# A first image load whose reads span two rows (32 KB) in place of one (16 KB), without the build's mark, in a 3x3 convolution with a residual

## The chip, the cores and the metric

The kernel runs on one core of one Trainium2 chip. The metric is the device time of one execution in microseconds (us), as the median of several runs. "Slower" or "faster" is said of over 2%.

## The reference

Sixteen images of 64 channels and 64 x 64 pixels are convolved with 64 x 64 x 3 x 3 weights, padding 1, and a residual is added; all is float32.

```python
for b, co, ci, kh, kw in all indices:
    output[b, co] += weight[co, ci, kh, kw] * x_pad[b, ci, kh:kh+h, kw:kw+w]
return (output + residual).astype(np.float32)
```

In and out of HBM go 50.48 MB: images, residual and output of 16.78 MB each, and the weights.

## The kernel before

Images are handled in pairs: 128 partitions hold two images of 64 channels, one row of 16 KB each. ScalarE casts an image into a padded bfloat16 tile, TensorE multiplies, VectorE adds the residual, and SyncE stores. Two loads are moved to the very front of the program, ahead of its opening barrier (where all engines wait for each other): the first image pair on SyncE's DMA queue and the first residual pair on ScalarE's.

```python
def to_the_front(dma):
    ...
    front.insert(at, copy.replace(ins, ins=[fixed(a) for a in ins.ins], outs=[fixed(a) for a in ins.outs]))

for p in range(NPAIR):                      # SyncE
    if p >= NXR:
        nc.sync.wait_ge(s_half, 2 * (p - NXR) + 3)
    if p == 0:
        to_the_front(load_x(p))             # xr0 <- images 0 and 1
        nc.sync.dma_start(out=wraw[:, :], in_=w_rows[:, :]).then_inc(s_w, 16)
    else:
        load_x(p)
    ...                                     # residual pairs, then the stores

to_the_front(load_ro(0, nc.scalar))         # ScalarE: ro <- residual pair 0
for n in range(B):
    ...                                     # wait for the pair, cast image n
```

All DMAs of this program carry a mark, `ant_dge_precooked`, which the build puts on a DMA of a simple shape.

Of the kernel before, what the change touches and what calls it, by code (L numbers as in the profile page):

```python
# [15 lines left out]
def kernel(  # L16
# [64 lines left out]
    def load_x(p):  # L81
        return nc.sync.dma_start(out=xr[p % NXR][:, :], in_=x_bc[128 * p : 128 * p + 128, :]).then_inc(s_x[p % NXR], 16)

    def load_ro(i, e):
        pairs, cols, _ = RES[i]
        if i >= NR:
            e.wait_ge(s_r[i % NR], 16 * (i // NR))
        return e.dma_start(out=ro[:, pairs, cols], in_=res_bc[:, pairs, cols]).then_inc(s_r[i % NR], 16)
# [24 lines left out]
            )  # L113
        )

    def to_the_front(dma):



        def fixed(ap):  # L120
            t = ap.bass_ap.tensor.name
            return mybir.PhysicalAccessPattern(
                ap=ap.ap, offset=ap.bass_ap.offset, dtype=ap.dtype, memref=t, memsetref=t + "_set", bass_ap=ap.bass_ap
            )

        front = nc.main_func.blocks[0].instructions
        here = nc.cur_bb.bb.instructions
        ins = here.pop()
        assert ins.name == dma.ins.name
        at = next(i for i, e in enumerate(front) if e.engine == ins.engine)  # L130
        front.insert(at, copy.replace(ins, ins=[fixed(a) for a in ins.ins], outs=[fixed(a) for a in ins.outs]))


    blocks = ((0, 0, 0, 0), (1, 0, 0, 1), (1, 0, 1, 0), (0, 1, 1, 1), (0, 1, 0, 2), (1, 1, 1, 2))
# [7 lines left out]
    with tc.tile_critical(no_gpsimd_drain=True):  # L142

        for p in range(NPAIR):
            if p >= NXR:

                nc.sync.wait_ge(s_half, 2 * (p - NXR) + 3)
            if p == 0:
                to_the_front(load_x(p))
                nc.sync.dma_start(out=wraw[:, :], in_=w_rows[:, :]).then_inc(s_w, 16)  # L150
            else:
                load_x(p)
            for i, (_, _, behind) in enumerate(RES):
                if behind == p:
                    load_ro(i, nc.sync)
# [24 lines left out]


        to_the_front(load_ro(0, nc.scalar))
        for n in range(B):
            p, im = divmod(n, 2)
            hp = slice(64 * im, 64 * im + 64)
            x4 = xr[p % NXR].rearrange("q (j two w) -> q j two w", two=2, w=W)
            t = xp[n % NXP]
# [22 lines left out]
        for n in range(B):  # L210
            p, im = divmod(n, 2)
# [81 lines left out]
```

## Time and profile before

| | before |
|---|---|
| time, median of the first 3 runs (122.21 to 122.33) | 122.28 us |
| span of the profiled run | 120.6 us |
| first DMA packet starts, last one ends | 1.03 us, 119.21 us |
| first image cast starts | 11.54 us |
| first convolution matmul starts | 18.12 us |

The prediction below shows the page's lines and reads from them that the 16 DMA engines have no free time between the first packet and the last. In such a kernel the end is the time at which the engines get going plus the bytes over the rate.

### The profile page before, as it was taken

To read this page: it belongs to the slowest core of one execution; us is meant where nothing else is said; L and a number is where in the kernel's file an instruction comes from. 1 tells how busy PE (TensorE), PEld (TensorE's weight loads), DVE (VectorE), ACT (ScalarE), POOL (GpSimd) and SP (SyncE) were. 2 spreads that over 40 slices of the span, in tenths; PEclk is the share of its full clock that TensorE was granted. 3 is DMA by queue.
4 is the path that set the end of the run, shared out by engine and by line. 5 is a ranking of instruction groups with operands and counts; after the bars stand their busy time and mean duration, and the time that the engine had idled before them with its cause. 6 is when DMAs were issued, how large, how long until landed. Compare 5 with 4: busy or idle time off the path is not lost.

```text
span 120.6 us, 734 instructions
## 1 busy us (share of the span) xinstructions
PE 87.7 (73%) x389; PEld 10.7 (9%) x105; DVE 76.0 (63%) x40; ACT 63.1 (52%) x37; POOL 2.4 (2%) x16
## 2 busy tenths in 40 slices
PE   0000609999999999999999999999999999400000
PEld 0000300111101110101010101010101010000000
DVE  0000080039898898988989898898988989890000
ACT  4001999999988595875959578595800000000000
POOL 5200000000000000000000000000000000000000
PEclk9999999999999999999999999999999999995555
DMA  7999999999999999999999999999999999999994
GB/s 239 429 424 429 430 429 429 429 435 435 435 429 429 424 429 424 429 435 424 435 429 435 435 435 418 421 459 435 429 429 429 429 429 435 435 435 429 399 427 168
DMA packets 3808, 50.48 MB, mean 419 GB/s; under 512 B 352, under 2 KB 480, under 8 KB 480
## 3 DMA queue, kind: packets, MB, share of 16 engines
q1 hardware_dynamic: 3664, 48.38, 94.2%
q10 hardware_dynamic: 144, 2.10, 4.1%
HBM read 33.70 MB, written 16.78 MB: 419 GB/s over the span
## 4 chain that ended last, share of the span: by engine, by line
PE 71%; DVEq 2%; DVE 2%; issue 0%
PE ps L101 54%; PE ps L100 17%; DVEq L142 2%; DVE ro L220 2%
## 5 line engine op out<-in xcount | busy, mean ns | idle before, releaser
L220 DVE TENSOR_TENSOR ro<-ps,ro 64x2048 f32<-64x2048 f32 x32 | 73.2, 2288 | 17.7 <-PE ps L101 17.2
L101 PE MATMUL ps<-xp,wl 128*128 128x504 bf16 (+1 forms) x288 | 80.0, 388 | 0.2
L190 ACT CAST xp<-xr 64x2048 bf16<-64x2048 f32 x16 | 30.3, 1896 | 22.5 <-PE ps L101 13.1
L100 PE MATMUL ps<-xp,wl 128*128 128x504 bf16 (+1 forms) x92 | 35.9, 390 | 3.4 <-PEq L241 3.4
L194 ACT CAST xp<-xr 64x2048 bf16<-64x2048 f32 x16 | 30.4, 1898 | 0.4
L100 PEld LDWEIGHTS ps<-xp,wl 128*128 128x128 bf16 x96 | 9.5, 99 | 79.1 <-issue 79.1
L206 DVE CAST wl<-ps 32x192 bf16<-32x192 f32 x8 | 2.8, 348 | 14.9 <-PE ps L233 14.8
L233 PE MATMUL ps<-ident,wraw 128*32 128x128 f32 x9 | 2.1, 412 | 12.6 <-DMA wraw<-in_weight_dram 12.6
L233 PEld LDWEIGHTS ps<-ident,wraw 128*32 128x32 f32 x9 | 1.2, 137 | 13.0 <-issue 12.6
L190 ACT ACT_TABLE_LOAD x1 | 1.3, 1283 | 1.1 <-SPq L142 1.1
L199 ACT CAST wl<-ps 32x192 bf16<-32x192 f32 x4 | 1.2, 306 | 0.0
L177 POOL MEMSET xp<- 64x64 bf16 x4 | 0.6, 146 | 0.2
L176 POOL MEMSET xp<- 64x64 bf16 x4 | 0.6, 144 | 0.2
L165 POOL TENSOR_SCALAR_AFFINE_SELECT ident<-ident 128x128 f32<-128x128 f32 x1 | 0.3, 292 | 0.2 <-POOL ident L163 0.2
L179 POOL MEMSET wl<- 64x192 bf16 x1 | 0.3, 253 | 0.1
L178 POOL MEMSET wl<- 64x192 bf16 x1 | 0.3, 251 | 0.1
L163 POOL MEMSET ident<- 128x128 f32 x1 | 0.2, 204 | 0.7 <-SPq L142 0.7
L277 POOL MEMSET const-bfloat16-1.0<- 128x1 bf16 x1 | 0.1, 111 | 0.0
L277 POOL MEMSET const-uint8-127<- 128x1 uint8 x1 | 0.1, 111 | 0.0
L277 POOL MEMSET const-float32-1.0<- 128x1 f32 x1 | 0.1, 108 | 0.0
L277 POOL MEMSET const-float32-0.0<- 128x1 f32 x1 | 0.1, 103 | 0.2 <-issue 0.2
## 6 DMA issues: line engine op xcount, KB each, us to landing
xr<-in_x_dram SPq DMA_DIRECT2D x8, 2048.0 KB, 14.4
out_dram<-ro SPq DMA_DIRECT2D x3, 4096.0 KB, 19.2
ro<-in_residual_dram SPq DMA_DIRECT2D x2, 4096.0 KB, 20.7
ro<-in_residual_dram SPq DMA_DIRECT2D x2, 2048.0 KB, 18.1
ro<-in_residual_dram ACTq DMA_DIRECT2D x1, 2048.0 KB, 12.0
ro<-in_residual_dram SPq DMA_DIRECT2D x2, 1024.0 KB, 18.8
out_dram<-ro SPq DMA_DIRECT2D x1, 2048.0 KB, 13.7
out_dram<-ro SPq DMA_DIRECT2D x2, 1024.0 KB, 9.4
```

Of the source, the lines that this page charges most:

```text
L100: return e.matmul(out=out_, lhsT=lhsT, rhs=rhs, start=start, stop=stop, skip_group_check=True)
L101: return e.add_instruction(mybir.InstMatmult(name=nc.get_next_instruction_name(), engine=PE, ins=[e.lower_ap(rhs), e.lower_ap(lhsT)], outs ...
L142: with tc.tile_critical(no_gpsimd_drain=True):
L176: nc.gpsimd.memset(t[0:64, 0, :], 0.0).then_inc(s_id, 1)
L177: nc.gpsimd.memset(t[64:128, J, :], 0.0).then_inc(s_id, 1)
L190: i = nc.scalar.copy(out=t[64:128, 0:J, :], in_=x4[hp, :, 0, :])
L194: nc.scalar.copy(out=t[0:64, 1 : J + 1, :], in_=x4[hp, :, 1, :]).then_inc(s_pack, 1)
L199: i = nc.scalar.copy(**weight_block(h, *b))
L206: i = nc.vector.tensor_copy(**weight_block(h, *b))
L220: i = nc.vector.tensor_tensor(out=o4[hp, :, par, :], in0=psj[64 * par : 64 * par + 64, :, :], in1=o4[hp, :, par, :], op=ADD)
L233: i = nc.tensor.transpose(out=tp[0:32, t // 3, 128 * (t % 3) : 128 * (t % 3) + 128], in_=wraw3[:, :, t], identity=ident[:, :])
L277: nc = _bacc.Bacc("TRN2", target_bir_lowering=False, num_devices=1)
```

## The change

The intent: each DMA engine takes turns between the two queues, one packet each. If a packet of the image's queue carries 32 KB instead of 16, the image gets two thirds of the engines' time instead of half and arrives sooner. The new shape is not one that the build marks, so the change clears the mark on this one load.

```diff
-    def to_the_front(dma):
+    def to_the_front(dma, wide=False):
 ...
+        if wide:
+            (step, rows), *mid, (_, cols) = src.ap
 ...
+            src = copy.replace(src, ap=[[2 * cols, rows // 2], [1, 1], [1, 2 * cols]])
+            dst = copy.replace(dst, ap=[list(dst.ap[0]), [1, 1], list(dst.ap[-1])])
-        front.insert(at, copy.replace(ins, ins=[fixed(a) ...], outs=[fixed(a) ...]))
+        front.insert(at, copy.replace(ins, ins=[src], outs=[dst], ant_dge_precooked=not wide))
 ...
-                to_the_front(load_x(p))
+                to_the_front(load_x(p), wide=True)
```

More of the change, by code (lines that the diff above doesn't have):

```diff
@@ L114, in matmul, with fixed @@
         )
-    def to_the_front(dma):
-        def fixed(ap):
-            t = ap.bass_ap.tensor.name
-            return mybir.PhysicalAccessPattern(
-                ap=ap.ap, offset=ap.bass_ap.offset, dtype=ap.dtype, memref=t, memsetref=t + "_set", bass_ap=ap.bass_ap
-            )
+    def fixed(ap):
+        t = ap.bass_ap.tensor.name
+        return mybir.PhysicalAccessPattern(
+            ap=ap.ap, offset=ap.bass_ap.offset, dtype=ap.dtype, memref=t, memsetref=t + "_set", bass_ap=ap.bass_ap
+        )
+    def to_the_front(dma, wide=False):
         front = nc.main_func.blocks[0].instructions
@@ L129, in to_the_front @@
         assert ins.name == dma.ins.name
+        (src,), (dst,) = ins.ins, ins.outs
+        src, dst = fixed(src), fixed(dst)
+        if wide:
+            (step, rows), *mid, (_, cols) = src.ap
+            assert step == cols and all(n == 1 for _, n in mid)
+            src = copy.replace(src, ap=[[2 * cols, rows // 2], [1, 1], [1, 2 * cols]])
+            dst = copy.replace(dst, ap=[list(dst.ap[0]), [1, 1], list(dst.ap[-1])])
         at = next(i for i, e in enumerate(front) if e.engine == ins.engine)
-        front.insert(at, copy.replace(ins, ins=[fixed(a) for a in ins.ins], outs=[fixed(a) for a in ins.outs]))
+        front.insert(at, copy.replace(ins, ins=[src], outs=[dst], ant_dge_precooked=not wide))
     blocks = ((0, 0, 0, 0), (1, 0, 0, 1), (1, 0, 1, 0), (0, 1, 1, 1), (0, 1, 0, 2), (1, 1, 1, 2))
```

## The prediction

> **What bounds the kernel now.** I read the chain of waits first, because it names a suspect, and then the DMA rows, to see whether the suspect can be right. In the page, part 4 is the chain that ended last, part 2 the slices; the tenths of the DMA row are the mean busy share of the 16 DMA engines.
>
> ```profile
> PE   0000609999999999999999999999999999400000
> ...
> DMA  7999999999999999999999999999999999999994
> GB/s 239 429 424 429 430 429 429 429 435 435 435 429 429 424 429 424 429 435 424 435 429 435 435 435 418 421 459 435 429 429 429 429 429 435 435 435 429 399 427 168
> ...
> HBM read 33.70 MB, written 16.78 MB: 419 GB/s over the span
> ## 4 chain that ended last, share of the span: by engine, by line
> PE 71%; DVEq 2%; DVE 2%; issue 0%
> ```
>
> The chain says TensorE, but it ends near 108.9 us, when the last two stores are issued. What follows is transfer. The DMA row is at 9 from the second slice to the last but one, and PE is idle for the first four slices and the last five. I checked this on the records of single packets: all 16 engines run their packets back to back from 1.03 us (first packet) to 119.21 us (end of the last), each 16 KB packet in 611 ns, and no gap appears anywhere between. So the span is 1.03 us of start, 118.18 us of transfer, and 1.4 us of completion and closing barrier (119.21 to 120.61). The time of 122.28 us is 1.67 us more than the span.
>
> The second question is how much room the compute chain has before it would set the end. The last stores are issued at 108.88 and 109.28 us. The records show 4.19 MB whose packets start after 108.88 us; 2.10 MB of that are these two stores, so 2.10 MB stand ahead of them: at 0.43 MB per us, 4.9 us. Compute could end almost 5 us later before a DMA engine went idle, and ending earlier gains nothing.
>
> Then the start, where the change is. Stretches of the timeline (start, duration, engine, line):
>
> ```profile
> 0.00 0.38 SPq L82 DMA_DIRECT2D xr<-in_x_dram  x1
> 0.12 0.36 ACTq L88 DMA_DIRECT2D ro<-in_residual_dram  x1
> ...
> 1.11 0.33 SPq L150 DMA_DIRECT2D wraw<-in_weight_dram  x1
> ...
> 11.54 1.90 ACT L190 CAST xp<-xr 64x2048 bf16<-64x2048 f32 x1 [9.19 <-DMA xr<-in_x_dram]
> ...
> 12.61 2.08 PE L233 MATMUL ps<-ident,wraw 128*32 128x128 f32 x9 [12.61 <-DMA wraw<-in_weight_dram]
> 13.46 1.90 ACT L194 CAST xp<-xr 64x2048 bf16<-64x2048 f32 x1
> 14.80 2.89 DVE L206 CAST wl<-ps 32x192 bf16<-32x192 f32 x8 [14.80 <-PE ps L233]
> 15.27 1.26 ACT L199 CAST wl<-ps 32x192 bf16<-32x192 f32 x4
> ...
> 18.12 0.59 PE L100 MATMUL ps<-xp,wl 128*128 128x512 bf16 x1 [3.44 <-PEq L241]
> ```
>
> The reader is to see which of two loads opens the convolution. The image lands at 11.5 us and both its casts end at 13.46 + 1.90 = 15.36 us. The weights land at 12.47 us, are transposed until 14.69 us and cast by VectorE until 14.80 + 2.89 = 17.69 us; the first convolution matmul follows 0.43 us later. The weights set the first matmul; the image is 2.3 us early already.
>
> The packet records also show how the first image shares the engines with the first residual load, which ACT issues 0.12 us later. Each engine takes two image packets (starts at 1.03 to 1.56 and 2.10 to 2.64 us), then one of the residual (from 2.73), and from there strictly one and one. The image's eighth packet on the leading engine ends at 10.09 us; its completion write gets a turn only after another residual packet, at 10.69 us. The 128 weight packets (1152 bytes, 51 ns) run after that, 11.30 to 12.16 us.
>
> **What the Trainium skill says.** All four are on "DMA: Bandwidth & Descriptors".
> (1) Section "Queues, rings and completion order": each DMA engine goes round its queue rows at packet granularity. The trace agrees (the alternation above). If a 32 KB descriptor counts as one packet, the image takes two thirds of each round in place of a half.
> (2) Section "Bandwidth", "Where 436 GB/s comes from": the ceiling is 435 GB/s. The slices of the trace lie at 424 to 435, so there is no rate left to gain.
> (3) Section "Why a DMA increments its semaphore by 16 and not by 1": the number of engines k is the largest number up to 16 that divides the slowest dimension of both patterns. Here these become 64 on the source and 128 on the destination, so k stays 16. No trace shows this shape yet.
> (4) Section "Latency and other measured facts": first byte of an issue from SyncE or ScalarE some 600 ns. The trace has 0.65 us from the end of SyncE's first issue (0.38) to its first packet (1.03).
> I found nothing on these pages about the "precooked" mark that the change takes off this one load.
>
> **The change part by part.**
> *Removed:* per engine, 4 of 8 read descriptors of one load. Residual halves of 8 KB take 309 ns, and 2 x 309 - 611 = 7 ns, which I take as the fixed cost of a descriptor. 4 x 7 = 28 ns per engine: -0.03 us on the transfer, which is on the path.
> *Added:* every DMA in the program before carries the mark; this one loses it. What an unmarked issue costs on SyncE no run here shows. The eight image loads' issues last 327 to 562 ns; I take this spread, 0.24 us, as an estimate of what a slower issue may add. It would move the first packet from 1.03 to about 1.25 us. There is a cap: ACT's issue ends at 0.48 us, and with the same 0.65 us its packets could begin at 1.13 us, 0.10 us after the present start; the engines would then begin with residual packets instead. So the engines start 0.1 to 0.24 us later; I take +0.15 us, on the path. SyncE's longer issue also delays the opening barrier, hence the weights' issue (1.11 us), but their packets wait in the queue until after 9 us anyway: 0.
> *Moved:* with 32 KB rounds the image needs 8 packets of its own and about 3 of the residual, in place of 7 at the end of before (6 between, 1 before the completion write): 4 x 0.61 = 2.4 us less at most, 1.8 us if one more round slips in, minus the later start. I expect the image to land at about 9.5 us (9 to 10.3) instead of 11.5. The residual is not later: both loads together are the same 16 packets per engine. The weights stand behind the image in SyncE's queue. If they go round one descriptor at a time with the residual's remaining 4 or 5 packets, the last weight packet still follows the last residual packet, and they land at 12.3 to 12.7 us, as before. ScalarE then casts image 0 about 2 us sooner and waits for the transposes; VectorE still ends its weight casts near 17.7 us, and the first convolution matmul stays at 18.0 to 18.4 us. On the end: 0, for two reasons, as the weights gate the matmuls and the DMA engines gate the end.
> *Sum:* 122.28 + 0.15 - 0.03 + 0 = 122.40 us.
>
> **The rivals.**
> Compute sets the end, as the chain of waits suggests, and an image that lands 2 us earlier takes up to 2 us off: about 120.3 us. Against it: 4.9 us of queued transfer ahead of the last store, and no DMA gap in 118 us. Even if true, the weights hold the first matmul.
> The weights come earlier: if several weight descriptors go in one turn, they land near 10 us, and the first matmul moves to about 15.7 us. That is a real move of the compute chain, but the same 50.48 MB follow: 122.4 us again. The image loads that wait for ScalarE would be issued earlier into a queue that is never empty.
> The wide descriptor is bad for the engines: the two patterns differ in length, so the load runs at half its rate or on fewer engines. Its 2.1 MB cost 4.9 us of the 16 engines; at half rate, with the residual filling in only partly, 1 to 4 us would be lost: 123.5 to 126 us. For: no run here has such a shape. Against: the page's rule keeps 16 engines, and 16 KB packets already run at the ceiling.
> The unmarked issue is far slower, 1 us or more: the residual's 4.9 us of work is there to fill in, so the loss stays near 0.25 us: 122.5 us.
>
> **Range and chances.** Three of these ways end within 122.25 to 122.55 us; the spread of the runs of before (122.21 to 122.33) and the 0.4 us by which the engines' last packets differ (118.78 to 119.21) widen it. The range is 122.15 to 122.75 us. Faster by over 2% needs under 119.9 us, less than the transfer with its start and closing takes: 0.01. Slower by over 2% needs over 124.7 us, which only the bad-descriptor way gives: 0.02. Within 2%: 0.97.
>
> **What would show it.** The first packet at 1.1 to 1.3 us, and the last packet's end shifted by about the same; the DMA row still without a gap; 64 fewer packets, if a packet is a read descriptor; ScalarE's first cast at 9.3 to 10.4 us in place of 11.54; the transposes at 12.4 to 12.9 us; the first convolution matmul at 18.0 to 18.4 us. I am wrong if the time moves by more than 0.5 us either way, if a DMA slice in the first 12 us falls below 9, or if the first matmul moves with the image. The weakest step is the cost of the missing mark.

## The result, and the profile after

The changed kernel takes 122.79 us (median of 4 runs, 122.67 to 122.98), the kernel before 122.31 us in the same rounds. The ratio is 1.0042 with a 95% interval of 1.0024 to 1.0059. Ratios here are the mean time of one kernel's runs over that of the other's of the same rounds, so not quite the ratio of the medians quoted. It is within 2%, as forecast, but the time lies 0.04 us outside the range, and the rise is 0.48 us where 0.12 was named.

First the page's slice rows after. One slice is 3.03 us, and a packet is booked in the slice in which it starts.

```profile
DMA  6989999999999999999999999999999999999993
GB/s 179 514 357 387 447 433 433 433 433 433 428 433 433 428 433 433 433 433 433 433 428 433 433 433 398 433 458 433 433 428 422 433 428 433 433 428 433 409 422 160
DMA packets 3744, 50.48 MB, mean 417 GB/s; under 512 B 352, under 2 KB 480, under 8 KB 480
```

The engines are full from the second slice on. The digit of 8 in the third comes from the booking: with each packet's time spread over its duration, the records fill that slice. The loss lies at the left edge: the first slice has 179 GB/s where it had 239. The 64 packets that are missing (3744 after 3808) are the wide load's: 64 of 32 KB in place of 128 of 16 KB. The single 514 and 357 are no real rates: a 32 KB packet is booked whole where it starts.

Then the opening in the timeline after (start, duration, engine, line):

```profile
0.00 0.56 SPq L82 DMA_DIRECT2D xr<-in_x_dram  x1
0.12 0.38 ACTq L88 DMA_DIRECT2D ro<-in_residual_dram  x1
...
1.43 0.36 SPq L157 DMA_DIRECT2D wraw<-in_weight_dram  x1
...
11.77 1.90 ACT L197 CAST xp<-xr 64x2048 bf16<-64x2048 f32 x1 [9.10 <-DMA xr<-in_x_dram]
...
12.85 2.08 PE L240 MATMUL ps<-ident,wraw 128*32 128x128 f32 x9 [12.85 <-DMA wraw<-in_weight_dram]
...
15.04 2.89 DVE L213 CAST wl<-ps 32x192 bf16<-32x192 f32 x8 [15.04 <-PE ps L240]
15.49 1.26 ACT L206 CAST wl<-ps 32x192 bf16<-32x192 f32 x4
...
18.36 0.59 PE L100 MATMUL ps<-xp,wl 128*128 128x512 bf16 x1 [3.44 <-PEq L248]
```

SyncE's issue takes 0.56 us instead of 0.38, and all that follows the opening barrier is later (the weights' issue at 1.43 us, before 1.11). The first cast of the image starts at 11.77 us: the image lands later than before, not sooner. The chain of transposes, weight casts and first matmul is 0.24 us later throughout.

The page does not show single packets, but the trace has their records. Chained by their times into engines, four of the 16 open like this (start us, duration us, KB, S for SyncE's queue and A for ScalarE's):

```
before  1.03 1.07 16 S   2.10 0.79 16 S   2.88 0.63 16 A   3.51 0.61 16 S
before  1.18 1.47 16 S   2.64 0.61 16 S   3.24 0.64 16 A   3.88 0.61 16 S
after   1.22 1.58 16 A   2.79 0.61 16 A   3.40 0.64 16 A   4.04 1.21 32 S
after   2.16 0.71 16 A   2.86 0.61 16 A   3.47 0.63 16 A   4.09 1.22 32 S
```

Two things changed. ScalarE's queue now opens, and gives three packets on each engine before SyncE's first. And the opening is slower: first packets last longer (mean 1.17 us after 1.08), and three engines get their first packet only after 2 us. To put a number on it I spread each packet's bytes evenly over its duration and sum what had been moved by 4.0 us: 966 KB before, 812 KB after (in these sums a KB is 1000 bytes; a packet of 16 KB has 16384). At 430 KB per us the missing 154 KB are 0.36 us. The mean over the 16 engines of the end of the last packet moved by 0.34 us (118.935 to 119.273), the very last by 0.42 (119.21 to 119.64), the span by 0.42. So nearly all was lost by 4.0 us, and the remaining 117 us neither gave any back nor lost much more.

### The profile page after: what moved, and what is told of

It is laid out like the page before. It is cut to its first block, busy times and chain, and to the rows that moved or that the text cites. A ratio compares the mean times of both kernels' runs of the same rounds, so it can differ in the third digit from the quotient of the medians.

```text
span 121.0 us, 734 instructions
## 1 busy us (share of the span) xinstructions
PE 87.2 (72%) x389; PEld 10.6 (9%) x105; DVE 76.0 (63%) x40; ACT 63.1 (52%) x37; POOL 2.4 (2%) x16
## 2 busy tenths in 40 slices
DMA packets 3744, 50.48 MB, mean 417 GB/s; under 512 B 352, under 2 KB 480, under 8 KB 480
## 4 chain that ended last, share of the span: by engine, by line
PE 70%; DVEq 2%; DVE 2%; issue 0%
PE ps L101 53%; PE ps L100 17%; DVEq L149 2%; DVE ro L227 2%
## 6 DMA issues: line engine op xcount, KB each, us to landing
ro<-in_residual_dram SPq DMA_DIRECT2D x2, 2048.0 KB, 18.4
```

## The experiments

All kernels gave right results. The columns of the table are from the packet records of one profiled execution each. "Moved" is what had been moved 3.0 us after the kernel's own first packet, so that a later start does not count in it. "Second queue" is the first packet of the queue that does not open. Each ratio uses the runs of before in its own rounds, whose medians lay between 122.31 and 122.55 us.

| kernel | first packet | second queue | moved, KB | time, us | ratio (95%) |
|---|---|---|---|---|---|
| before | 1.03 | 2.73 | 977 | 122.31 | 1 |
| after | 1.15 | 3.62 | 877 | 122.79 | 1.0042 (1.0024 to 1.0059) |
| e1 narrow, unmarked | 1.15 | 3.48 | 867 | 122.80 | 1.0036 (1.0023 to 1.0049) |
| e2 ScalarE's load unmarked | 1.03 | 5.00 | 787 | 122.80 | 1.0035 (1.0022 to 1.0047) |
| e3 after, ScalarE behind | 1.34 | 5.77 | 813 | 123.21 | 1.0066 (1.0053 to 1.0079) |
| e4 before, SyncE behind | 1.15 | 5.18 | 816 | 122.87 | 1.0049 (1.0036 to 1.0061) |
| e5 before, ScalarE behind | 1.01 | 5.04 | 783 | 122.83 | 1.0047 (1.0027 to 1.0066) |
| e10 as e5, ScalarE far later | 1.01 | 11.63 | 817 | 122.79 | 1.0030 (1.0017 to 1.0044) |
| e11 before, both behind | 1.94 | 2.93 | 970 | 123.63 | 1.0091 (1.0074 to 1.0108) |
| e12 second queue small | 1.01 | 2.90 | 818 | 123.38 | 1.0073 (1.0059 to 1.0087) |
| e8 roles swapped | 1.01 | 2.69 | 954 | 122.40 | 1.0001 (0.9989 to 1.0014) |
| e9 both queues, one tensor | 1.01 | 2.71 | 961 | 122.30 | 0.9998 (0.9985 to 1.0011) |
| e7 wide on nine later loads | 1.02 | 2.71 | 974 | 122.45 | 1.0008 (0.9995 to 1.0021) |
| e13 half a residual pair first | 1.03 | 2.41 | 990 | 122.47 | 0.9999 (0.9986 to 1.0013) |

My first theory was that the loss is the missing mark: the longer issue on SyncE lets ScalarE's queue open, and that queue opens slowly. The rivals were the 32 KB packet itself, and an unmarked issue that slows the engines whichever queue it is on. Four runs on one chip were to tell them apart.

**e1: the mark alone.**

```diff
-                to_the_front(load_x(p), wide=True)
+                to_the_front(load_x(p), marked=False)   # 16 KB rows
```

> The first image load keeps its 16 KB rows and only loses the mark. If the missing mark is the cause (a longer issue on SyncE, so that ScalarE's queue opens): issue about 0.55 us, the residual's packets first, time 122.7 to 122.9 us, a ratio of about 1.004. If the 32 KB descriptor is the cause: issue about 0.55 us but the time at most 0.15 us above before (122.3 to 122.45).

Measured: 122.80 us, and an opening like that of the changed kernel.

```profile
DMA  5999999999999999999999999999999999999994
GB/s 173 433 433 393 452 428 433 433 423 433 428 433 433 433 433 433 433 433 433 428 433 428 433 433 406 431 463 423 428 433 417 433 428 428 433 428 433 414 431 173
```

The first slice has 173 GB/s, with no 32 KB packet in the program. The width is not the cause; the missing mark is enough.

**e2: the mark taken from ScalarE's load instead.**

```diff
-        to_the_front(load_ro(0, nc.scalar))
+        to_the_front(load_ro(0, nc.scalar), marked=False)
```

> As before, but ScalarE's first residual load loses the mark instead. If what costs is that ScalarE's queue opens: SyncE still opens, so no change, 122.2 to 122.4 us. If an unmarked issue slows the start of the DMA engines whichever queue it is on: 122.5 to 122.8 us.

```profile
0.00 0.38 SPq L82 DMA_DIRECT2D xr<-in_x_dram  x1
0.12 0.52 ACTq L88 DMA_DIRECT2D ro<-in_residual_dram  x1
```

ScalarE's issue lasts 0.52 us instead of 0.36. SyncE opens at 1.03 us as before, and still 122.80 us. That ScalarE's queue opens is thus not what costs: the first theory, in this form, fell. ScalarE's first packet comes only at 5.00 us.

**e3: the changed kernel with ScalarE's load out of the way.**

```diff
-        to_the_front(load_ro(0, nc.scalar))
+        load_ro(0, nc.scalar)                           # behind the barrier
```

> The changed kernel, with ScalarE's first residual load issued behind the opening barrier, so that SyncE's wide load opens alone. First packet at about 1.2 us. If the loss lay in the order (ScalarE's queue opens): only the longer issue is left, +0.15 to +0.2 us, 122.45 to 122.55 us, first image landed by 9.5 us. If the unmarked issue itself starts the engines slowly: 122.7 us or more.

Measured: 123.21 us, the slowest so far. The queue order was not the trouble: with SyncE opening alone it got worse, not better. Against the hope of 122.5 us this run is a miss, and the first packet at 1.34 us was later than the 1.2 expected.

**e4: before, with SyncE's load out of the way.**

```diff
-                to_the_front(load_x(p))
+                load_x(p)                               # behind the barrier
```

> The kernel before with the first image load marked, narrow and issued behind the opening barrier, so that ScalarE's queue opens with no SyncE load beside it. First packet about 0.1 us later than before. If ScalarE's queue opens slowly by itself: 122.65 to 122.9 us. If the slow opening needs SyncE's unmarked load beside it: 122.35 to 122.5 us.

Measured: 122.87 us. No unmarked load is in this kernel, and it opens as slowly (816 KB). What e1 to e4 and the changed kernel share is that only one queue has packets in the first 3.4 us. So I formed a second theory, BOTH: the engines come up to full rate sooner when both queues have large packets waiting in the first microseconds; anything that keeps one of them away costs some 0.4 us. The rival, DISTURBED, was that the making of a load's descriptors (the orders for its single stretches of bytes) at the wrong moment slows the first packets.

**e5: before, with ScalarE's load out of the way.**

```diff
-        to_the_front(load_ro(0, nc.scalar))
+        load_ro(0, nc.scalar)
```

> The kernel before (narrow, marked first load) with ScalarE's first residual load issued behind the opening barrier: SyncE's queue opens alone at about 1.03 us, and no unmarked issue is anywhere. Theory BOTH (the engines reach their full rate late when only one queue has descriptors for them in the first microseconds): under 850 KB moved by 4.0 us where before has 966 KB, time 122.65 to 122.95 us. Theory DISTURBED (an unmarked issue slows the engines while its descriptors are made): no loss, some 950 KB, 122.3 to 122.45 us.

```profile
DMA  6999999999999999999999999999999999999994
GB/s 168 422 433 400 450 428 433 433 433 433 428 433 433 433 433 433 428 428 433 433 433 433 433 433 404 422 463 433 433 428 428 433 428 428 433 422 433 404 433 176
```

122.83 us: SyncE's narrow, marked load starts as early as before (1.01 us), and the first slice has 168 GB/s. By 4.0 us 778 KB had been moved, which is under the 850 that BOTH had named. DISTURBED falls in the form that needs an unmarked issue.

**e8: the roles swapped.** SyncE issues the residual pair, ScalarE the image.

```diff
-        return nc.sync.dma_start(out=xr[p % NXR][:, :], ...
+        return (nc.scalar if p == 0 else nc.sync).dma_start(out=xr[p % NXR][:, :], ...
-        to_the_front(load_ro(0, nc.scalar))
+        to_the_front(load_ro(0, nc.sync))
```

> The kernel before with the roles of the two opening queues swapped: SyncE issues the residual load, ScalarE the image load, both narrow, marked and early. Theory BOTH, and DISTURBED too: as before, 122.25 to 122.45 us. A theory that the residual's load is itself a slow opener (its rows lie 128 KB apart in on-chip memory): 122.65 us or more.

```profile
GB/s 234 418 429 429 435 434 429 429 424 434 429 429 434 424 424 434 429 434 429 429 434 434 434 429 415 432 451 429 429 429 434 434 429 429 429 434 434 407 424 168
```

As before: 234 GB/s in the first slice, ratio 1.0001. Neither the residual's layout nor which queue carries it matters.

**e9: two queues, one tensor.** ScalarE opens with the second image pair instead of the residual.

```diff
-        to_the_front(load_ro(0, nc.scalar))
+        to_the_front(load_x(1))                         # issued by ScalarE
+            elif p == 1:
+                load_ro(0, nc.sync)
```

> The kernel before, but ScalarE's opening load is the second image pair in place of the first residual pair, which SyncE issues in the image's old place: two queues at the start, but both read the same tensor. Theory BOTH as a matter of queues: as before, 122.25 to 122.45 us. If it is a matter of two tensors in HBM being read at once: 122.65 us or more.

Ratio 0.9998. That two tensors are read is not what makes the opening fast. Two queues and two loads still go together here: each of them has a load of its own, from its own stretch of HBM.

**e7: the width where the queue is full.**

```diff
+            else:
+                widen(load_x(p))                        # image pairs 3 to 6
+                    if i > 1 and RES[i][1] is WHOLE:
+                        widen(d)                        # residual pairs 2 to 6
```

> First image load as before (narrow, marked); image loads 3 to 6 and residual pairs 2 to 6 wide and unmarked (the two residual loads of two pairs split in two each), so that the longer issue is hidden behind a full queue. Nine loads of 4 wide packets per engine, each 9 ns shorter than two narrow ones (1213 against 2 x 611): 9 x 4 x 9 = 0.32 us less, 121.95 to 122.15 us. If the width gains nothing on a full queue: 122.3 to 122.45 us.

This was the attempt at a version that beats both: the wide loads' longer issue hidden, the width kept. Measured 122.45 us, ratio 1.0008: no loss, and no gain where 0.32 us had been named. The sum that it rested on was wrong. The records give 1213 ns for a 32 KB packet against 611 for 16 KB, but records of neighbours overlap by some 4 ns: packets of 16 KB start 607 ns apart, those of 32 KB 1209 or 1210. Two narrow ones cost 1214 ns, a wide one 1210, so nine loads save 9 x 4 x 4 = 144 ns, not 324. The interval, from 0.06 us faster to 0.26 us slower, does not show even that.

**e10: ScalarE's load only after the image.** In e5 ScalarE issues its load at about 1.1 us, among the first packets; here it waits for the image.

```diff
             if im == 0:
                 nc.scalar.wait_ge(s_x[p % NXR], 16 * (p // NXR + 1))
+            if n == 0:
+                load_ro(0, nc.scalar)
```

> As e5, but ScalarE issues its residual load only when the first image has landed, so that no other issue of ScalarE falls into the opening. Theory BOTH: as e5, 700 to 850 KB by 4.0 us, 122.65 to 123.0 us. If in e5 it was ScalarE's issue at about 1.1 us, during the first packets, that slowed SyncE's: 930 KB or more, 122.25 to 122.45 us.

122.79 us and 812 KB by 4.0 us: slow, with no issue on ScalarE anywhere near. That leaves nothing of DISTURBED as far as ScalarE is concerned.

**e11: both loads behind the barrier.**

```diff
-                to_the_front(load_x(p))
+                load_x(p)
-        to_the_front(load_ro(0, nc.scalar))
+        load_ro(0, nc.scalar)
```

> The kernel before with both opening loads behind the opening barrier, each marked and narrow. The first packet then starts near 2.1 us, 1.1 us later. Theory BOTH: the same ramp from there on, so about 1.1 us longer in all, 123.3 to 123.6 us. A rival, WARM (the memory serves slowly until some 2.5 us after the program's start, whoever asks): the ramp is short now and the loss under 0.8 us, 122.8 to 123.15 us.

The first packet starts at 1.94 us, 0.91 us later (1.1 had been named), and from there the opening is that of before: 970 KB in 3.0 us after 977. The mean end of the engines moved by 0.94 us, and the ratio of 1.0091 is 1.1 us; the 123.63 us are 0.03 above the range named. So the slow opening is not tied to the program's first 2.5 us. It also shows what bringing the two loads to the front is worth.

**e12: a second queue with small packets.** ScalarE opens with the weights, whose rows are 1152 bytes.

```diff
-        to_the_front(load_ro(0, nc.scalar))
+        to_the_front(nc.scalar.dma_start(out=wraw[:, :], in_=w_rows[:, :]).then_inc(s_w, 16))
-                nc.sync.dma_start(out=wraw[:, :], in_=w_rows[:, :]).then_inc(s_w, 16)
+                load_ro(0, nc.sync)
+                nc.sync.dma_start(out=spare[0:16, :], in_=w_rows[0:16, :]).then_inc(s_out, 16)
```

> The kernel before with ScalarE's opening load being the weights (128 rows of 1152 bytes) in place of the residual, which SyncE issues in the weights' old place (and 16 rows of the weights once more into a spare buffer, 18 KB, which the build needs). If a second queue as such makes the opening fast: 122.25 to 122.45 us. If it has to bring large packets: 122.65 to 122.95 us. In both cases weights and image land by 8 us and the first convolution matmul moves from 18.1 to about 12.5 us, 5 to 6 us sooner, and that alone takes nothing off the time, as the DMA engines set the end.

```profile
8.04 1.90 ACT L192 CAST xp<-xr 64x2048 bf16<-64x2048 f32 x1 [5.69 <-DMA xr<-in_x_dram]
...
8.81 2.08 PE L235 MATMUL ps<-ident,wraw 128*32 128x128 f32 x9 [8.81 <-DMA wraw<-in_weight_dram]
...
11.00 2.89 DVE L208 CAST wl<-ps 32x192 bf16<-32x192 f32 x8 [11.00 <-PE ps L235]
...
14.33 0.58 PE L101 MATMUL ps<-xp,wl 128*128 128x512 bf16 x1 [3.44 <-PEq L243]
```

The opening is slow (818 KB), so a second queue as such is not enough. And the first convolution matmul starts at 14.33 us, 3.8 us sooner than before (I had named 12.5, and both landings by 8 us), while the time rises: an earlier start of the convolution takes nothing off. The 123.38 us lie outside both ranges: the rise of 0.9 us is more than the opening explains. Between 10 and 75 us most packets of 16 KB last 612 to 619 ns in this kernel and 611 before; some 3.7 ns more in the mean on about 106 packets per engine is another 0.4 us. Why, I did not test.

**e13: the wide, unmarked load kept, behind two quick openers.**

```diff
             if p == 0:
-                to_the_front(load_x(p), wide=True)
+                to_the_front(load_ro(5, nc.sync))       # 1 MB of the last residual pair
+                widen(load_x(p))                        # still 32 KB and unmarked
-        wait_ro(nc.sync, len(RES) - 2)
+        wait_ro(nc.sync, 4)
```

Each residual load also got a semaphore of its own.

> The wide, unmarked first image load stays, but SyncE's opening place goes to a marked load of half a residual pair (1 MB, 8 KB packets), which no later work waits for; the wide load follows behind the opening barrier. ScalarE opens as before. Theory BOTH: both queues have descriptors early again, 900 KB or more by 4.0 us, 122.2 to 122.5 us, although the image lands later than before (12 to 13.5 us) and the first convolution matmul at 18 to 19.5 us. If the wide unmarked load costs its time wherever it stands: 122.65 us or more.

```profile
DMA  6999999999999999999999999999999999999993
GB/s 217 413 500 435 386 435 429 435 435 418 429 429 435 429 435 435 429 429 429 418 429 435 435 435 435 410 459 435 429 429 435 435 424 435 429 429 424 410 429 160
```

```profile
0.00 0.39 SPq L88 DMA_DIRECT2D ro<-in_residual_dram  x1
0.12 0.36 ACTq L88 DMA_DIRECT2D ro<-in_residual_dram  x1
...
1.13 0.55 SPq L82 DMA_DIRECT2D xr<-in_x_dram  x1
...
14.54 1.90 ACT L210 CAST xp<-xr 64x2048 bf16<-64x2048 f32 x1 [12.18 <-DMA xr<-in_x_dram]
...
20.53 0.58 PE L100 MATMUL ps<-xp,wl 128*128 128x512 bf16 x1 [3.44 <-PEq L261]
```

The wide load's issue lasts 0.55 us here too, but behind the barrier, where SyncE's first packets are already on their way and ScalarE's load has been issued (its first packet starts at 2.41 us). By 4.0 us 978 KB have gone, and the time is that of before (0.9999), though the first matmul starts 2.4 us later than before. (The image's cast at 14.54 us and this matmul came later than the 12 to 13.5 and 18 to 19.5 us named.) The cost does not belong to the wide load. It belongs to being the opener. (The first slice's 217 is not lower in substance: its 8 KB and 32 KB packets are booked where they start.)

No run beat the kernel before. The table falls in two groups with nothing between them: 954 to 990 KB where the second queue's large packets begin within 1.8 us of the first packet, and 783 to 877 KB where they begin after 2.3 us or more, or are small. And the bytes account for the end: in every kernel but e12 the later first packet plus the missing KB at 430 KB per us give the shift of the engines' mean end to within 0.06 us (e3: 0.31 + 0.38 against 0.69 us; e11: 0.91 + 0.02 against 0.94).

Three things are still open. The first is what the engines do in those microseconds. The groups part before the second queue has moved anything: 1.5 us after the first packet the fast kernels have moved 340 to 361 KB and the slow ones 246 to 291, while in before and e7 to e9 the second queue's first packet comes only 1.68 to 1.70 us after it. So the second load acts while it waits, and the records do not say how. The length of the first packets alone does not tell the groups apart: its mean is 1.34 us in e5 and 1.08 before, but 1.17 in both the slow changed kernel and the fast e9. The second is whether it takes two queues, or only two large loads at once: two early loads on one queue, or one load split over both, were not tried. The third is why an unmarked load that was issued early, as in e1, counts as one that is missing; its late first packet (3.48 us) suggests it, but no run shows what happens in between. Nor was a wide load with the mark tried.

## Why the prediction was wrong

*What bounds the kernel.* Right. The DMA engines set the end: a first matmul 3.8 us sooner (e12) or 2.4 us later (e13) took nothing off and added nothing, while the changes of the opening came out at the end (in e12 with more that stays unexplained).

*The term that failed* is "So the engines start 0.1 to 0.24 us later; I take +0.15 us, on the path." Its first half held: the issue grew by 0.17 us, ScalarE's packets stepped in, and the first packet moved by 0.12 us, from 1.03 to 1.15. But I took the start of the first packet for the start of the transfer and let the ramp behind it (the first microseconds, until the engines move their full rate) be as before. In that ramp the engines moved 877 KB in 3.0 us instead of 977; 100 KB at 430 KB per us are 0.23 us. With the 0.12 this makes 0.35; the engines' mean end moved by 0.34. The rest, up to the 0.42 of the last packet, is the spread between engines. The same step led me to call the longer issue capped ("the loss stays near 0.25 us"): one queue filling in for the other keeps the engines busy, but it does not bring them up as fast. The prediction's own reading held a sign of the ramp: it has the first packets start at 1.03 to 1.56 us and the second at 2.10 to 2.64, over 1 us apart, and yet counts each packet as 611 ns.

*The gain of fewer descriptors* (-0.03 us) was too large, as the records of e7 showed: 4 wide packets save 4 x 4 = 16 ns. It changes nothing. Two other readings were loose, also without effect: of the full slices some lie outside 424 to 435 (399 to 459), and the first engine to end does so at 118.72 us, not 118.78.

*The image.* Expected at about 9.5 us; its cast started at 11.77. Packets of 32 KB do get twice the share: from 3.6 us on the records alternate strictly between 1213 ns of S and 611 of A. But the image starts three residual packets late, as its queue no longer opens. I had that case in view as the cap on the start, and did not carry it into the image's time.

*The weights gate the first matmul.* Right: transposes at 12.85 us (12.4 to 12.9 named), first matmul at 18.36 (18.0 to 18.4).

*The rivals and the signs.* All sixteen engines carried the wide load, as the rule under (3) of the prediction has it, and the wide packet ran at full rate, so the bad-descriptor way did not occur. The range was too narrow because every way that I placed inside it shared the assumption about the ramp. Of the signs named, the first packet, the 64 fewer packets, the transposes and the first matmul held. The first cast did not, nor did the last packet's end: it shifted by 0.42 us where the first packet moved by 0.12. The sign of being wrong that did show, a digit of 8 in the third slice, is an effect of the booking and points at nothing; the ramp lies in the first slice, which was below 9 before, too (7, then 6).

## What to carry to other kernels

This is from one kernel, in which it was worth 0.4 to 1.1 us of 122. Where the DMA engines are full from first packet to last, look for the end's microseconds in the first four, and measure the bytes moved there, not the time of the first packet. Have large loads ready on both hardware queues as early as possible, and give the opening places to the loads that are quickest to issue; a load with a costlier form belongs one place behind. A DMA that lands sooner is worth nothing if what it feeds waits for another, or if the engines only change the order of the same bytes.

## What the Trainium skill lacked or had wrong

- "DMA: Bandwidth & Descriptors", section "Issuing engines are not separate DMA queues": it says that issuing from several engines only saves the sequencer's time. In the steady part that agrees with these runs (before: 424 to 429 GB/s in slices 2 to 4 with two queues, 424 to 435 in most later ones with one), but not in the opening: with an early load of 1 or 2 MB on each of two queues 954 to 990 KB went in the first 3.0 us after the first packet, with one on one queue 783 to 817 KB (e4, e5, e10), 0.4 to 0.6 us at the end.
- No page has the mark on a DMA that the build calls precooked. Without it an issue took 0.56 us on SyncE instead of 0.38, and 0.52 on ScalarE instead of 0.36; the drain that follows SyncE's issue ended at 0.98 us instead of 0.56, and the second queue's first packet came at 3.48 to 5.00 us instead of 2.73 (e1, e2, the changed kernel).
- The same page, section "Queues, rings and completion order": turns go packet by packet, and the runs agree, for 32 KB packets too (1213 ns against 611). It lacks that at the opening one queue gave two packets (before) or three (after) before the other got its turn, though both loads had been issued by 0.56 us.
- No page gives in time what packets over 16 KB gain: some 4 ns in 1214, and nothing measurable on 36 of them per engine (e7).
